# Values and transposed weights of key blocks with one query tile: split float32r products in shared banks

## The chip, the cores and the metric

The kernel runs on one core of a Trainium2 chip, as one program. The metric is the device time of one execution in microseconds. TensorE does the matrix products and the transposes and writes PSUM; ScalarE (ACT in the rows), VectorE (DVE) and GpSimd (POOL) do the rest; SyncE (SP) issues the transfers.

## What is computed

A trunk of two layers on 1024 tokens of width 1024. The first layer mixes tokens by dilated sliding-window attention: 16 heads of 64, and three groups with a window and a dilation each; the groups' outputs are merged by a softmax over their log-sum-exps. The second layer is a state-space layer with its own projections. All inputs and outputs are float32. The part that matters:

```python
DILATED_GROUPS = ((128, 1), (512, 4), (2048, 16))
def dilated_group_attention(q, k, v, rel_bias, window, dilation):
    # query t attends to t - j*dilation, j = 0..window/dilation
    ...
    logits = jnp.einsum('bnqrhe,bnkrhe->bnrhqk', qs, kw) * scale + bias
    logits = jnp.where(valid[None, :, None, None], logits, NEG)
    lse = jax.nn.logsumexp(logits, axis=-1)
    p = jnp.exp(logits - lse[..., None])
    o = jnp.einsum('bnrhqk,bnkrhe->bnqrhe', p.astype(v.dtype), vw)
    ...
def dilated_attention_mixer(h, w_in, w_out, rel_bias):
    ...
    wts = jax.nn.softmax(jnp.stack(lses), axis=0)
    o = jnp.sum(wts[..., None] * jnp.stack(outs).astype(jnp.float32), axis=0)
    ...
    return (o * jax.nn.silu(z)) @ w_out
```

## The kernel before

The program has stages one after the other: norm and values of all groups, written to DRAM (until some 343 us of the profiled span); attention (343 to 1165 us); gate and output projection; the state-space layer; its gate and the last projection.

Attention runs over 8 pairs of heads (`attn_pair`, L665), in each over the three groups, in each over two units of four query tiles of 128 (`attn_unit`, L472). For a group, queries and keys are projected (`proj_half`, L114; the products stand on L110), brought out of PSUM and split. To split (`split`, L79) means: ScalarE writes a tile rounded to float32r (L83), VectorE or GpSimd subtracts it from the source to get the rest (L84). A product of near float32 precision is then made of two or three float32r products of the parts.

`load_v` (L444) brings the values of a pair and group, eight key blocks of 128 tokens with two heads of 64, from DRAM into `vp` (L454; two buffers) and splits them into `vs` (one buffer): rounded part in 64 columns, rest in the next 64, so one product with 128 columns of weights gives both halves, and the two halves of the result are added when it leaves PSUM (L582, L583). In groups 0 and 1 only the blocks listed in `SPLIT_BLOCKS` (L226) are split: six of eight in group 0, four in group 1. These are the blocks that serve two query tiles of a unit.

In a unit, the logits of a query tile are products of the split queries and keys (L495), 256 columns wide, or 128 where a query tile has a single key block. VectorE adds the bias and takes the row maximum (L498), ScalarE takes the exponential (L509). Then `pv_first` (groups 0 and 1) or `pv_last` (group 2) makes the products with the values. `pv_first` goes head by head: blocks of weights are transposed by TensorE into a PSUM bank (`transposed`, L516; pool of two banks, tile `pt`), the bank is split into `ph` (`split_weights`, L524; two buffers), and each key block with two query tiles gets two products of 256 columns, rounded and rest, with `vs` (L572). Key blocks with one query tile in the unit are transposed into a bank of their own (tile `ptp`), copied by ScalarE to the float32 tile `pf` (L568) and multiplied with the raw `vp` as plain float32 products with 64 columns of weights and 128 columns (L572 too, operands `pf,vp`). In a unit and head these are two key blocks (unit 0 of group 0, both units of group 1) or one (unit 1 of group 0). All products of a head and unit accumulate in one bank, in the order of the list `jobs`.

The order on each engine is set at build time: a scheduler takes ready instructions by priority along a simulated time line, and some steps (weight loads and splits, evictions of projections) are put ahead by `AHEAD`. On the chip each engine and the SP queue keep that order and wait by semaphores. Weights of a projection come through `load_w` (L90, load on L95), the bias tile through `load_bias` (L180, L186).

Of the kernel before, what the change touches and what calls it, by code (L numbers as in the profile page):

```python
# [15 lines left out]
F32 = mybir.dt.float32  # L16
F32R = mybir.dt.float32r
# [6 lines left out]
P = 128  # L24
S = 1024
D = 1024
KT = 8
H = 512
# [192 lines left out]
        c.nc.gpsimd.tensor_copy(t[rows, s, :], c.zt[rows].to_broadcast([64, S]))  # L221

SPLIT_BLOCKS = ((0, 1, 2, 4, 5, 6), (0, 2, 4, 6), (0, 1, 2, 3, 4, 5, 6, 7))  # L226


def load_first(c, a, k):
    raw = c.wraw.tile([P, 2, H], F32, tag="wraw", name="wvr")  # L230
    c.nc.sync.dma_start(raw, a["w_v"][0, k // 2])
# [212 lines left out]
def load_v(c, p, g):  # L444


    nc = c.nc
    vp = c.attn.tile([P, KT, P], F32, tag="vp", name="vp", bufs=2)
    o = ORD[g]
    off = c.v_dr.offset + (g * 2 + p // 4) * S * H + p % 4 * P  # L450

    for dst, at, step in (((vp, 0, P),), ((vp[:, 0::2], 0, 1), (vp[:, 1::2], o * P, 1)), ((vp, 0, 1),))[g]:
        src = bass.AP(c.v_dr.tensor, off + at * H, [[o * H, P], [step * H, dst.shape[1]], [1, P]])
        nc.sync.dma_start(dst, src)  # L454
    vs = c.attn.tile([P, KT, 2, P], F32R, tag="vs", name="vs", bufs=1)
    if g == 2:
        split(c, vs[:, :, 0], vs[:, :, 1], vp)
        return vp, vs
    src = vp.rearrange("p b (h d) -> p b h d", h=2)
    nb = len(SPLIT_BLOCKS[g])  # L460
    for n, blocks in enumerate((slice(0, 3), slice(4, 7)) if g == 0 else (slice(0, 8, 2),)):
        dst = vs[:, 3 * n:3 * n + 3] if g == 0 else vs[:, 0:nb]
        split(c, dst[:, :, :, 0:64], dst[:, :, :, 64:128], src[:, blocks])
    return vp, vs


def ms_col(g, n, h, qt):
# [4 lines left out]
def attn_unit(c, g, u, q, k, v, bt, ms, O):  # L472


    nc = c.nc
    qh, ql = q
    kh, kl = k
    vp, vs = v
    lg = c.attn.tile([P, 2, 4, 256], F32, tag="lg", name="lg", bufs=3)
    tiles = []  # L480
    for j in range(4):
        qt = u * 4 + j
        m = (7 - qt, 1 - qt % 2, 0)[g]
        start = (max(m - 1, 0) * P, qt // 2 * 256, qt * P)[g]
        w = 256 if m else 128
        tiles.append(w)
        ps = c.psl.tile([P, 2, 256], F32, tag="psl", name="psl")
        qs = slice(qt * P, qt * P + P)
        ks = slice(start, start + w)
        if g == 2:  # L490
            jobs = [(ps[:, :, 0:w], a, b[:, :, ks]) for a, b in ((qh, kh), (qh, kl), (ql, kh))]
        else:
            jobs = [(ps[:, h, 0:w], (qh, ql)[h], b[:, h, ks]) for h in range(2) for b in (kh, kl)]
        for n, (o, a, b) in enumerate(jobs):
            nc.tensor.matmul(o, a[:, qs], b, start=n == 0, stop=n == len(jobs) - 1, skip_group_check=True)  # L495
        for h in range(2):
            col = ms_col(g, 0, h, qt)
            nc.vector.tensor_tensor_reduce(  # L498
                lg[:, h, j, 0:w], ps[:, h, 0:w], bt[:, h, 256 - w:256], scale=1.0, scalar=-3.0e38,
                op0=ALU.add, op1=ALU.max, accum_out=ms[:, col:col + 1])  # L500
    nm = c.small.tile([P, 2, 4], F32, tag="nm", name="nm")
    at = (4 - 4 * u, 4 * u, 4 * u)[g]
    mx = ms[:, 0:16].rearrange("p (h t) -> p h t", h=2)[:, :, at:at + 4]
    nc.vector.tensor_scalar(nm, mx, -1.0, None, op0=ALU.mult)  # L504
    for h in range(2):
        for j, w in enumerate(tiles):
            col = ms_col(g, 1, h, u * 4 + j)
            b = (3 - j, j ^ 1, j)[g]
            nc.scalar.activation(lg[:, h, j, 0:w], lg[:, h, j, 0:w], AF.Exp, bias=nm[:, h, b:b + 1],  # L509
                                 accum_out=ms[:, col:col + 1])  # L510
    (pv_last if g == 2 else pv_first)(c, g, u, lg, vp, vs, O)
    if u == 1:
        put_ms(c, g, ms)


def transposed(c, lg, blocks, name):  # L516

    pt = c.pst.tile([P, H], F32, tag="pst", name=name)
    for n, (h, j, part) in enumerate(blocks):
        c.nc.tensor.transpose(pt[:, n * P:(n + 1) * P], lg[:, h, j, part * P:part * P + P], c.ident)  # L520
    return pt


def split_weights(c, pt, wd):  # L524
    t = c.attn.tile([P, 2, H], F32R, tag="ph", name="ph", bufs=2)
    hi, lo = t[:, 0], t[:, 1]
    split(c, hi[:, 0:wd], lo[:, 0:wd], pt[:, 0:wd])
    return hi, lo
# [9 lines left out]
    return O[g]  # L538


def pv_first(c, g, u, lg, vp, vs, O):


    nc = c.nc

    if g == 0:
        sp = [(6 - 4 * u - j, j, [(j, 0), (j + 1, 1 if j < 2 or u == 0 else 0)]) for j in range(3)]
        pl = [(7 - 4 * u, 0, [(0, 1)])]
        if u == 0:
            pl.append((3, 3, [(3, 0)]))  # L550
    else:
        sp = [(4 * u + j, j, [(j, 0), (j + 1, 0)]) for j in (0, 2)]
        pl = [(4 * u + 1 + j, j, [(j, 1)]) for j in (0, 2)]
    for h in range(2):
        po = c.pso.tile([P, H], F32, tag="pso", name="pso")
        jobs = []
        for b0 in range(0, len(sp), 2):
            grp = sp[b0:b0 + 2]
            pt = transposed(c, lg, [(h, j, part) for _, _, parts in grp for j, part in parts], "pt")
            hi, lo = split_weights(c, pt, 256 * len(grp))  # L560
            for n, (kb, col, parts) in enumerate(grp):
                s = slice(256 * n, 256 * n + 256)
                for x in (hi, lo):
                    jobs.append((po[:, col * P:col * P + 256], vs[:, SPLIT_BLOCKS[g].index(kb), h], x[:, s]))
        pt = transposed(c, lg, [(h,) + parts[0] for _, _, parts in pl], "ptp")
        wd = P * len(pl)
        pf = c.slot("pf", F32, tag="a")
        nc.scalar.copy(pf[:, 0:wd], pt[:, 0:wd])  # L568
        for n, (kb, col, parts) in enumerate(pl):
            jobs.append((po[0:64, col * P:col * P + P], vp[:, kb, 64 * h:64 * h + 64], pf[:, n * P:(n + 1) * P]))  # L570
        for n, (o, l, r) in enumerate(jobs):
            nc.tensor.matmul(o, l, r, start=n == 0, stop=n == len(jobs) - 1, skip_group_check=True)  # L572
        out = out_tile(c, g, O)

        rows = HEADS[h]
        if g == 0:
            dst = out[rows].rearrange("p (i n) -> p i n", i=8)[:, :, 64 - 64 * u:128 - 64 * u]
            fr = [po[x, ::-1].rearrange("p (n i) -> p i n", i=8) for x in HEADS]
        else:
            dst = out[rows].rearrange("p (b r n) -> p r b n", b=2, r=4)[:, 2 * u:2 * u + 2]  # L580
            fr = [po[x].rearrange("p (r l) -> p r l", r=2)[:, :, ::-1].rearrange("p r (n b) -> p r b n", b=2) for x in HEADS]
        nc.scalar.copy(dst, fr[0])  # L582
        nc.vector.tensor_tensor(dst, dst, fr[1], op=ALU.add)  # L583


def pv_last(c, g, u, lg, vp, vs, O):


    nc = c.nc
# [1040 lines left out]
```

## Time and profile before

| | us |
|---|---|
| median of 3 runs | 1743.67 |
| lowest, highest | 1740.37, 1746.24 |
| profiled execution | 1741.3 |
| its span, first to last instruction | 1739.5 |
| TensorE busy over the span | 1677.0 (96%) |
| VectorE busy | 1038.2 (60%) |
| ScalarE busy | 797.3 (46%) |
| GpSimd busy | 482.1 (28%) |

The mean granted TensorE clock is 0.991 of full speed. Busy time of TensorE is a sum of modelled spans of products that overlap in the pipeline, so the starts of successive products tell more of its pace than their durations. In the rows, PE is TensorE's products and transposes, PEld its weight loads; L572 is line 572 of the kernel; `out<-in,in` are tiles by the program's names, the moving operand ahead of the weights.

### The profile page before, as it was taken

To read this page: it belongs to the slowest core of one execution; us is meant where nothing else is said; L and a number is where in the kernel's file an instruction comes from. 1 tells how busy PE (TensorE), PEld (TensorE's weight loads), DVE (VectorE), ACT (ScalarE), POOL (GpSimd) and SP (SyncE) were. 2 spreads that over 40 slices of the span, in tenths; PEclk is the share of its full clock that TensorE was granted. 3 is DMA by queue.
4 is the path that set the end of the run, shared out by engine and by line. 5 is a ranking of instruction groups with operands and counts; after the bars stand their busy time and mean duration, and the time that the engine had idled before them with its cause. 6 is when DMAs were issued, how large, how long until landed. Compare 5 with 4: busy or idle time off the path is not lost. (4 is left out here: it accounts for less than half of the span.)

```text
span 1739.5 us, 25821 instructions
## 1 busy us (share of the span) xinstructions
PE 1677.0 (96%) x9262; PEld 1414.2 (81%) x9262; DVE 1038.2 (60%) x2558; ACT 797.3 (46%) x1912; POOL 482.1 (28%) x321
## 2 busy tenths in 40 slices
PE   6999999999999999999999999998998999989998
PEld 5889999987878888788888888886886888867886
DVE  7698898634555556455564656467462677764533
ACT  5232222246656656666666756653352232233411
POOL 2000000132242332424253252405120344423121
PEclk9999999999999999999999999998999999999999
DMA  6223455441233223223232332427249866455432
GB/s 233 90 52 100 145 170 152 143 125 53 77 86 88 76 80 100 77 81 95 80 85 92 101 94 63 131 71 200 82 140 243 216 214 221 135 176 175 140 122 85
DMA packets 176900, 212.68 MB, mean 122 GB/s; under 512 B 37361, under 2 KB 133380, under 8 KB 176772
## 3 DMA queue, kind: packets, MB, share of 16 engines
q1 hardware_dynamic: 176772, 211.04, 40.7%
q8 instruction: 73, 1.20, 0.3%
q14 instruction: 55, 0.45, 0.1%
HBM read 154.03 MB, written 56.96 MB: 121 GB/s over the span
## 5 line engine op out<-in xcount | busy, mean ns | idle before, releaser
L110 PE MATMUL psj<-hh,whi 128*128 128x512 f32 x896 | 359.9, 402 | 7.3 <-DVE tz L814 3.8
L110 PE MATMUL psj<-hl,whi 128*128 128x512 f32 x896 | 357.5, 399 | 0.0
L110 PE MATMUL psj<-hh,wlo 128*128 128x512 f32 x896 | 356.3, 398 | 0.2 <-POOL wlo L84 0.2
L84 POOL TENSOR_TENSOR wlo<-wraw,whi 128x1024 fp32r<-128x1024 f32 x48 | 115.3, 2402 | 377.5 <-ACT whi L83 365.3
L110 PEld LDWEIGHTS psj<-hh,whi 128*128 128x128 f32 x896 | 169.4, 189 | 43.6 <-ACT kh L214 5.9
L110 PEld LDWEIGHTS psj<-hh,wlo 128*128 128x128 f32 x896 | 169.3, 189 | 36.4 <-POOL wlo L84 0.6
L110 PEld LDWEIGHTS psj<-hl,whi 128*128 128x128 f32 x896 | 169.6, 189 | 32.5
L509 ACT ACTIVATE lg<-lg,nm 128x128 f32<-128x128 f32 (+1 forms) x384 | 168.0, 440 | 22.9 <-DVE nm L504 22.2
L498 DVE CUSTOM_DVE_ANT_0 lg<-psl,T 128x128 f32<-128x128 f32 (+1 forms) x384 | 117.3, 348 | 91.1 <-PE psl L495 89.2
L83 ACT CAST whi<-wraw 128x1024 fp32r<-128x1024 f32 x80 | 83.8, 1048 | 147.0 <-PE psj L110 105.1
L394 PE MATMUL psq<-whi,v 128*128 128x256 f32 x640 | 118.7, 283 | 0.0
L110 PE MATMUL psj<-h1h,whi 128*128 128x512 f32 (+1 forms) x272 | 107.4, 395 | 11.3 <-DVE z L1415 7.9
L84 DVE TENSOR_TENSOR kl<-psj,kh 64x512 fp32r<-64x512 f32 x96 | 66.0, 687 | 76.0 <-ACT kh L83 75.7
L84 DVE TENSOR_TENSOR ph<-pt,ph 128x512 fp32r<-128x512 f32 (+1 forms) x128 | 78.7, 621 | 52.8 <-ACT ph L83 51.5
L110 PE MATMUL psj<-h1l,whi 128*128 128x512 f32 (+1 forms) x272 | 105.8, 389 | 0.2 <-DVE h1l L84 0.2
L110 PE MATMUL psj<-h1h,wlo 128*128 128x512 f32 (+1 forms) x272 | 105.4, 388 | 0.0
L394 PEld LDWEIGHTS psq<-whi,v 128*128 128x128 f32 x640 | 99.6, 189 | 1.0 <-ACT whi L83 0.6
L394 PE MATMUL psq<-wlo,v 128*128 128x256 f32 x320 | 90.7, 284 | 1.6 <-DVE wlo L84 1.6
L1231 POOL TENSOR_TENSOR Ks<-Ks,O 32x64 f32<-32x64 f32 x8 | 4.6, 572 | 296.8 <-ACT Ks L1229 281.1
L83 ACT CAST whi<-v 128x1024 fp32r<-128x1024 f32 x35 | 36.8, 1052 | 101.5 <-PE psq L394 74.2
L897 POOL TENSOR_TENSOR xr<-xr,y 128x512 f32<-128x512 f32 x30 | 38.1, 1292 | 139.0 <-DVE y L896 100.3
L520 PE MATMUL pt<-identr,lg 128*128 128x128 f32 x448 | 75.3, 278 | 0.2 <-ACT lg L509 0.2
(292 smaller groups left out, 4013.3 us busy)
## 6 DMA issues: line engine op xcount, KB each, us to landing
wraw<-in_w_in_dram SPq DMA_DIRECT2D x56, 512.0 KB
mw<-wt_dr SPq DMA_DIRECT2D x48, 256.0 KB
v<-in_w_v_dram SPq DMA_DIRECT2D x20, 512.0 KB
vp<-v_dr SPq DMA_DIRECT2D x16, 512.0 KB
wraw<-in_ssm_w_in_dram SPq DMA_DIRECT2D x16, 512.0 KB
v_dr<-v SPq DMA_DIRECT2D x30, 256.0 KB
rot_dr<-rt SPq DMA_DIRECT2D x48, 128.0 KB
ca_dr<-ca SPq DMA_DIRECT2D x32, 144.0 KB
```

Of the source, the lines that this page charges most:

```text
L83: nc.scalar.copy(hi, src)
L84: return (engine or nc.vector).tensor_tensor(lo, src, f32(hi), op=ALU.subtract)
L110: nc.tensor.matmul(ps, a[:, s], b[:, k, :], start=first and k == 0 and n == 0, stop=k == KT - 1 and n == 2, skip_group_check=True)
L394: nc.tensor.matmul(o, r[x][:, k, ts], w[y][:, k, :], skip_group_check=True, start=i in (0, 4, 5) and t % 2 == k == n == 0, stop=k == 3 and ...
L498: nc.vector.tensor_tensor_reduce(lg[:, h, j, 0:w], ps[:, h, 0:w], bt[:, h, 256 - w:256], scale=1.0, scalar=-3.0e38, op0=ALU.add, op1=ALU.m ...
L509: nc.scalar.activation(lg[:, h, j, 0:w], lg[:, h, j, 0:w], AF.Exp, bias=nm[:, h, b:b + 1], accum_out=ms[:, col:col + 1])
L520: c.nc.tensor.transpose(pt[:, n * P:(n + 1) * P], lg[:, h, j, part * P:part * P + P], c.ident)
L897: nc.gpsimd.tensor_tensor(x[:, ns], x[:, ns], y, op=ALU.add)
L1231: nc.gpsimd.tensor_tensor(Ks[:, :, 0:16], Ks[:, :, 0:16], self.dd, op=ALU.add)
```

## The change

Every key block of groups 0 and 1 is now split, in one piece of 1024 columns for each part, as in group 2; `SPLIT_BLOCKS` goes. Key blocks with one query tile are multiplied as split products: two float32r products of 128 columns with `vs` take the place of one plain product with `vp`. Their transposed weights go through the same eviction (`split_weights`) as the others: in group 0 they share the second bank with the third block of two tiles (512 columns in unit 0, 384 in unit 1), in group 1 they have the second bank to themselves (256 columns). The tiles `ptp` and `pf` are gone. `ph` gets three buffers in place of two, `vp` one in place of two.

```diff
--- before.py
+++ after.py
@@ -219,11 +219,6 @@
     for s in range(2):
         rows = HEADS[1 - s]
         c.nc.gpsimd.tensor_copy(t[rows, s, :], c.zt[rows].to_broadcast([64, S]))
-
-
-
-
-SPLIT_BLOCKS = ((0, 1, 2, 4, 5, 6), (0, 2, 4, 6), (0, 1, 2, 3, 4, 5, 6, 7))
 
 
 def load_first(c, a, k):
@@ -445,7 +440,7 @@
 
 
     nc = c.nc
-    vp = c.attn.tile([P, KT, P], F32, tag="vp", name="vp", bufs=2)
+    vp = c.attn.tile([P, KT, P], F32, tag="vp", name="vp", bufs=1)
     o = ORD[g]
     off = c.v_dr.offset + (g * 2 + p // 4) * S * H + p % 4 * P
 
@@ -455,13 +450,9 @@
     vs = c.attn.tile([P, KT, 2, P], F32R, tag="vs", name="vs", bufs=1)
     if g == 2:
         split(c, vs[:, :, 0], vs[:, :, 1], vp)
-        return vp, vs
-    src = vp.rearrange("p b (h d) -> p b h d", h=2)
-    nb = len(SPLIT_BLOCKS[g])
-    for n, blocks in enumerate((slice(0, 3), slice(4, 7)) if g == 0 else (slice(0, 8, 2),)):
-        dst = vs[:, 3 * n:3 * n + 3] if g == 0 else vs[:, 0:nb]
-        split(c, dst[:, :, :, 0:64], dst[:, :, :, 64:128], src[:, blocks])
-    return vp, vs
+    else:
+        split(c, vs[:, :, :, 0:64], vs[:, :, :, 64:128], vp.rearrange("p b (h d) -> p b h d", h=2))
+    return vs
 
 
 def ms_col(g, n, h, qt):
@@ -475,7 +466,6 @@
     nc = c.nc
     qh, ql = q
     kh, kl = k
-    vp, vs = v
     lg = c.attn.tile([P, 2, 4, 256], F32, tag="lg", name="lg", bufs=3)
     tiles = []
     for j in range(4):
@@ -508,7 +498,7 @@
             b = (3 - j, j ^ 1, j)[g]
             nc.scalar.activation(lg[:, h, j, 0:w], lg[:, h, j, 0:w], AF.Exp, bias=nm[:, h, b:b + 1],
                                  accum_out=ms[:, col:col + 1])
-    (pv_last if g == 2 else pv_first)(c, g, u, lg, vp, vs, O)
+    (pv_last if g == 2 else pv_first)(c, g, u, lg, v, O)
     if u == 1:
         put_ms(c, g, ms)
 
@@ -522,7 +512,7 @@
 
 
 def split_weights(c, pt, wd):
-    t = c.attn.tile([P, 2, H], F32R, tag="ph", name="ph", bufs=2)
+    t = c.attn.tile([P, 2, H], F32R, tag="ph", name="ph", bufs=3)
     hi, lo = t[:, 0], t[:, 1]
     split(c, hi[:, 0:wd], lo[:, 0:wd], pt[:, 0:wd])
     return hi, lo
@@ -538,36 +528,33 @@
     return O[g]
 
 
-def pv_first(c, g, u, lg, vp, vs, O):
+def pv_first(c, g, u, lg, vs, O):
 
 
     nc = c.nc
 
     if g == 0:
-        sp = [(6 - 4 * u - j, j, [(j, 0), (j + 1, 1 if j < 2 or u == 0 else 0)]) for j in range(3)]
-        pl = [(7 - 4 * u, 0, [(0, 1)])]
+        first = [(6 - 4 * u - j, j, [(j, 0), (j + 1, 1 if j < 2 or u == 0 else 0)]) for j in range(3)]
+        single = [(7 - 4 * u, 0, [(0, 1)])]
         if u == 0:
-            pl.append((3, 3, [(3, 0)]))
+            single.append((3, 3, [(3, 0)]))
+        banks = [first[:2], first[2:] + single]
     else:
-        sp = [(4 * u + j, j, [(j, 0), (j + 1, 0)]) for j in (0, 2)]
-        pl = [(4 * u + 1 + j, j, [(j, 1)]) for j in (0, 2)]
+        banks = [[(4 * u + j, j, [(j, 0), (j + 1, 0)]) for j in (0, 2)],
+                 [(4 * u + 1 + j, j, [(j, 1)]) for j in (0, 2)]]
     for h in range(2):
         po = c.pso.tile([P, H], F32, tag="pso", name="pso")
         jobs = []
-        for b0 in range(0, len(sp), 2):
-            grp = sp[b0:b0 + 2]
-            pt = transposed(c, lg, [(h, j, part) for _, _, parts in grp for j, part in parts], "pt")
-            hi, lo = split_weights(c, pt, 256 * len(grp))
-            for n, (kb, col, parts) in enumerate(grp):
-                s = slice(256 * n, 256 * n + 256)
+        for bank in banks:
+            blocks = [(h, j, part) for _, _, parts in bank for j, part in parts]
+            wd = P * len(blocks)
+            hi, lo = split_weights(c, transposed(c, lg, blocks, "pt"), wd)
+            at = 0
+            for kb, col, parts in bank:
+                n = P * len(parts)
                 for x in (hi, lo):
-                    jobs.append((po[:, col * P:col * P + 256], vs[:, SPLIT_BLOCKS[g].index(kb), h], x[:, s]))
-        pt = transposed(c, lg, [(h,) + parts[0] for _, _, parts in pl], "ptp")
-        wd = P * len(pl)
-        pf = c.slot("pf", F32, tag="a")
-        nc.scalar.copy(pf[:, 0:wd], pt[:, 0:wd])
-        for n, (kb, col, parts) in enumerate(pl):
-            jobs.append((po[0:64, col * P:col * P + P], vp[:, kb, 64 * h:64 * h + 64], pf[:, n * P:(n + 1) * P]))
+                    jobs.append((po[:, col * P:col * P + n], vs[:, kb, h], x[:, at:at + n]))
+                at += n
         for n, (o, l, r) in enumerate(jobs):
             nc.tensor.matmul(o, l, r, start=n == 0, stop=n == len(jobs) - 1, skip_group_check=True)
         out = out_tile(c, g, O)
@@ -583,7 +570,7 @@
         nc.vector.tensor_tensor(dst, dst, fr[1], op=ALU.add)
 
 
-def pv_last(c, g, u, lg, vp, vs, O):
+def pv_last(c, g, u, lg, vs, O):
 
 
     nc = c.nc
```

## Rows read from the trace of the kernel before

**Rows 1.** Windows: stretch, its length; busy us (count) by engine; clock; DMA share, GB/s.

```profile
343.00:1165.00 822.00, 812.35 (x4416) 675.84 (x4415) 432.73 (x1308) 508.67 (x1410) 293.32 (x163) 1.00 0.31 88
```

**Rows 2.** Waits of TensorE in 343:1165: who waits <- for whom, total us, times, longest.

```profile
PE pso L572 <- ACT ph L83: 4.2, 3, 1.9
```

**Rows 3.** Lines by shape, 343:1165: group, xcount | busy us, mean ns | idle before it.

```profile
L572 PEld LDWEIGHTS pso<-ph,vs 128*128 128x128 f32 x320 | 49.9, 191 | 9.4 <-ACT ph L83 4.8
...
L572 PEld LDWEIGHTS pso<-pf,vp 128*64 128x64 f32 x224 | 22.7, 136 | 12.3 <-issue 4.1 <-ACT kh L83 1.1 <-ACT pf L568 0.7
```

**Rows 4.** TensorE's timeline at 599 and 619 us: start, us, operation, xcount of merged records.

```profile
599.39 0.39 PE L110 MATMUL psj<-hl,whi 128*128 128x512 f32 x1
599.62 0.40 PE L110 MATMUL psj<-hh,wlo 128*128 128x512 f32 x1
599.95 0.65 PE L572 MATMUL pso<-pf,vp 128*64 128x128 f32 x4
600.53 0.44 PE L520 MATMUL pt<-identr,lg 128*128 128x128 f32 x2
...
619.62 0.43 PE L572 MATMUL pso<-pf,vp 128*64 128x128 f32 x2
619.98 0.44 PE L520 MATMUL pt<-identr,lg 128*128 128x128 f32 x2
```

**Rows 5.** TensorE's timeline at 623 us, logits of a tile with one key block.

```profile
623.42 0.22 PE L495 MATMUL psl<-kh,qh 128*128 128x128 f32 x1
623.48 0.28 PE L495 MATMUL psl<-kl,qh 128*128 128x128 f32 x1
623.59 0.28 PE L495 MATMUL psl<-kh,ql 128*128 128x128 f32 x1
623.70 0.27 PE L495 MATMUL psl<-kl,ql 128*128 128x128 f32 x1
623.81 0.45 PE L110 MATMUL psj<-hh,whi 128*128 128x512 f32 x1
```

**Rows 6.** Lines by shape, 343:1165: evictions of transposed weights, splits of values.

```profile
L84 DVE TENSOR_TENSOR ph<-pt,ph 128x512 fp32r<-128x512 f32 x95 | 65.2, 688 | 50.8 <-ACT ph L83 49.8
...
L83 ACT CAST ph<-pt 128x512 fp32r<-128x512 f32 x95 | 55.3, 585 | 13.4 <-PE pt L520 12.0
...
L568 ACT COPY pf<-ptp 128x256 f32<-128x256 f32 x48 | 17.9, 373 | 6.3 <-PE ptp L520 6.0
...
L84 DVE TENSOR_TENSOR ph<-pt,ph 128x256 fp32r<-128x256 f32 x32 | 13.5, 421 | 1.8 <-ACT ph L83 1.4
L83 ACT CAST ph<-pt 128x256 fp32r<-128x256 f32 x32 | 11.9, 372 | 0.2
L84 DVE TENSOR_TENSOR vs<-vp,vs 128x1024 fp32r<-128x1024 f32 x8 | 11.3, 1409 | 2.3 <-ACT vs L83 2.2
...
L83 ACT CAST vs<-vp 128x1024 fp32r<-128x1024 f32 x8 | 8.4, 1044 | 1.8 <-PE pso L572 1.8
...
L84 DVE TENSOR_TENSOR vs<-vp,vs 128x512 fp32r<-128x512 f32 x8 | 6.1, 765 | 24.0 <-ACT vs L83 24.0
L83 ACT CAST vs<-vp 128x512 fp32r<-128x512 f32 x8 | 4.9, 617 | 2.9 <-PE pso L572 2.9
```

**Rows 7.** Timeline, first pair, from group 0's last products to group 1's first.

```profile
423.01 0.28 PE L572 MATMUL pso<-ph,vs 128*128 128x256 f32 x1
...
423.98 0.69 DVE L84 TENSOR_TENSOR vs<-vp,vs 128x512 fp32r<-128x512 f32 x1 [2.51 <-ACT vs L83]
...
425.82 0.43 PE L572 MATMUL pso<-pf,vp 128*64 128x128 f32 x2
...
431.77 0.28 PE L572 MATMUL pso<-ph,vs 128*128 128x256 f32 x1
```

**Rows 8.** Timeline: SP's loads of values, and the next split of group 0.

```profile
459.23 2.04 SPq L454 DMA_DIRECT2D vp<-v_dr  x3
...
477.55 1.02 DVE L84 TENSOR_TENSOR vs<-vp,vs 128x384 fp32r<-128x384 f32 x2
```

## The prediction

> **What bounds the kernel now.** Only the attention stretch, 343 to 1165 us of the span, runs the code that is changed, so I read that stretch first, in the view that sums each engine over a window. TensorE is busy for 812 of its 822 us at the full granted clock, ScalarE for 509, VectorE for 433, GpSimd for 293 [rows 1]. The reader is to see one engine without room and three with a third or more to spare. A busy TensorE may be waiting between pipelined products, so next comes the list of its waits in that stretch: the longest is 4.2 us, on the ScalarE half of a split of transposed weights [rows 2]. All its idle time there is 10 us [rows 1]. So what counts is how long TensorE takes to issue its stream, and the starts of successive products are the measure, not their durations, which overlap.
>
> **The plain products that go.** For each of 8 pairs the two first groups have, per head and unit, one run of plain float32 products with 64 columns of weights. By the loops that is 6 runs of two products and 2 runs of one in a pair, 48 and 16 in the kernel, 112 products. The trace shows each product as two records, 224 of them [rows 3]. The neighbouring 512-column products start 0.23 us apart; from the last of them to the run of two there are 0.33 us, and from the run's start to the next instruction 0.58 us [rows 4]. So a run of two takes 0.33 - 0.23 + 0.58 = 0.68 us of TensorE. A run of one takes 0.36 us from its start [rows 4], and with the same 0.10 us ahead of it 0.46 us. Sum: 48 x 0.68 + 16 x 0.46 = 40.0 us.
>
> **The split products that come.** Each plain product becomes two float32r products of 128 columns, with all 128 columns of weights: four in a run where there were two, two where there was one, 224 in all. The same shape exists in the logits of the tiles with a single key block: four in a row start 0.06, 0.11 and 0.11 us apart, and the next instruction follows after another 0.11 us [rows 5]. The first one is short because its weights had come in behind a longer product; the others wait for theirs. A run of four takes 0.39 us, one of two 0.17 us: 48 x 0.39 + 16 x 0.17 = 21.4 us. If each paid 0.11 us it would be 24.6 us, if each were hidden behind longer products 0.06 x 224 = 13.4 us. I take 21.4, since the new runs follow 256-column products as those in the rows follow theirs. **TensorE gains 40.0 - 21.4 = 18.6 us**, with bounds of 15.4 and 26.6.
>
> The number of transposes stays at 560: blocks only move from a bank of their own into a shared one. That saves one bank in three in the first group, and the pool has two; it may relieve some of the waits, and I count nothing for it.
>
> **ScalarE and VectorE.** Per pair and head, the first unit of group 0 trades two ScalarE evictions of 256 columns (0.37 us each) for one wider part (0.59 in place of 0.37 us), so it saves 0.16 us; the second unit trades much the same; in group 1 a cast replaces the copy at the same price [rows 6]. ScalarE therefore stays where it was. VectorE gets work that did not exist: in group 1 a 256-column subtraction of 0.42 us for each of 32 heads and units; in group 0 subtractions that are wider by 256 columns (0.69 against 0.42) 16 times, and by 128, about half of that, 16 times. That is 13.4 + 4.3 + 2.1, about 20 us [rows 6]. The values are split in one piece of 1024 columns, also in group 1 (1.04 for 0.62 us on ScalarE, 1.41 for 0.77 on VectorE) [rows 6], which adds 8 x 0.64, some 5 us, to VectorE, and little in group 0, where two pieces become one. VectorE goes from 433 to about 460 of 822 us. As it is never what TensorE waits for by name [rows 2], I cost this at nothing. What hides it is TensorE's projection products of the next groups; uncovered, the 0.42 us at each of 64 units and heads would be 27 us.
>
> **The split values, one buffer.** They are written once TensorE has read the last of the group before. In the first pair the last split product of group 0 starts at 423.0, the last plain one at 425.8, as the plain one reads the raw values, not the split ones. After the change it reads the split values too, and the next split may begin only then, 2.8 us later. It is also longer by 0.43 + 0.64 us [rows 6], together 3.9 us. The subtraction ended at 424.7 and the next reader started at 431.8 [rows 7], 7.1 us later. In the eight pairs this slack is 3.1 to 7.1 us, and in six of them the release moves by about 0.5 us, not by 2.8. So it fits, and I cost it at nothing. Queued behind the split are, on ScalarE and VectorE, the exponentials and row maxima of the next unit.
>
> **The raw values, one buffer in place of two.** The load of a group now waits until the group before it has been split. Now three loads go out together at 459.2, two of them for group 1 of the next pair; after the change those two wait for the split of group 0, which ends at 478.6 [rows 8]. Group 1 needs them only after all of group 0's products, nearly 50 us later, so the landing is hidden. The queue is SP's, and weight and bias loads stand behind a load that waits. If the queue keeps its order, up to 478.6 - 459.2 = 19 us of a held queue would come in each pair; a weight load that far behind would stop TensorE for some of it. An order planned with the new wait puts the load later, so I take nothing. The third buffer for split weights only removes waits. Memory stays equal: one 4 KB buffer goes, one comes.
>
> **Sum.** The profiled execution's span is 1739.5 us and its own time 1741.3; 1741.3 - 18.6 = 1722.7 us. The median of the runs is 1743.67, 2.4 us more; on it the same sum gives 1725.1 us. I take **1725 us**.
>
> **A rule on weight loads.** The busy time of weight loads in the stretch is 676 of 822 us [rows 1], and the change puts 224 loads of 191 ns in place of 224 of 136 ns [rows 3], 12.3 us more. The Trainium skill, Perfetto Trace Analysis, section Identifying the Most-Contended Engine, judges TensorE's headroom by the busy share of weight loads and not by that of products. By that measure the change would be a loss. The first of the rivals below is this one, as a mechanism.
>
> **Rivals.**
> Weight side: if loads of weights set TensorE's pace everywhere, those 12.3 us come on top: 1756 us. Against it: loads of 0.19 us lie under products 0.23 us apart [rows 3, 4]; only in runs of 128 columns do they set the pace, and that is in the sum.
>
> Switching stays: at the column rate of the neighbours (0.23 us for 512) four passes of 128 columns take 0.23 us, two products 0.47, so 0.21 of the 0.68 us are entry and exit. If that belongs to the transposes that follow and not to the plain products, 64 x 0.21 = 13.4 us stay, the gain is 5.2 us and the time 1738.5. The four passes of a true float32 product are stated by the Trainium skill, FP8 and Floating Point Precision, section TensorE Precision Notes; the trace has two records, whose time goes beyond four passes. Against the rival: plain products add 0.10 us on entry already, before any transpose [rows 4].
>
> Handover of the split values, **the one that ends slower**: eight times, between groups 0 and 1, readers start 3.9 us later, 31 us in all, and 1743.7 - 18.6 + 31 = 1756 us. It decides once the delay exceeds the 3.1 to 7.1 us of slack, which happens if the new order puts the readers right behind the split as the old plan had it and VectorE's queue is full. Half exposed, 15.6 us, it gives 1741, no difference.
>
> More than the sum: products hidden at 0.06 us (26.6 us) and the 4.2 us of waits on the weights' split gone: some 31 us, 1713.
>
> **Chances.** Forecast, 1720 to 1730: 0.55. More than the sum, 1711 to 1720: 0.14. Switching stays, about 1738.5, on the edge of 0.3%: 0.06, half to each side. Handover or held queue half exposed, 1733 to 1748: 0.18, of which 0.05 on the fast side of 0.3%. Handover fully exposed: 0.05. Weight side: 0.02. About 0.3%, 5.2 us, is what a measurement of this kernel can tell from no change. Faster by over 0.3% (under 1738.4): 0.55 + 0.14 + 0.03 + 0.05 = 0.77. Within: 0.13 + 0.03 = 0.16. Slower: 0.05 + 0.02 = 0.07. The range goes from 1713, the far end of the gain, to 1741, the handover half exposed; some 0.15 lies above it and little below.
>
> **What would show it.** TensorE's records fall by 224 of the plain kind and rise by 224 of 128 columns; runs of the latter take 0.39 us or less and the stretch of attention shrinks by 15 to 27 us with TensorE still at 98% or more of it. The stages before and after keep their lengths to within 2 us. Wrong would be: new waits of TensorE on the split values or on VectorE's half of the split weights, a held SP queue with TensorE waiting for a weight split, or an attention stretch of about the old length with fewer busy microseconds in it.

## The result and the profile after

The changed kernel takes 1725.7 us (median of 4 runs, 1722.9 to 1727.7) against 1743.2 us before; the ratio is 0.9898, with a 95% interval of 0.9876 to 0.9921. The forecast was 1725. The sum holds nearly to the microsecond, but the profile shows that it is made of other parts than those I had added up, and most of what follows is about that.

Engines over the span, from the page of the kernel after:

```profile
span 1721.1 us, 25792 instructions
...
PE 1655.9 (96%) x9262; PEld 1415.1 (82%) x9262; DVE 1064.8 (62%) x2582; ACT 799.9 (46%) x1872; POOL 483.5 (28%) x321
```

VectorE has 26.6 us more in the whole span, ScalarE 2.6 us more, in line with the steps that cost them. The stretch of attention in the view by windows, which answers to [rows 1], is cut 18 us earlier here; the last product with values starts at 1156.2 us, 14.7 us earlier than before (1170.9):

```profile
343.00:1147.00 804.00, 792.30 (x4406) 676.93 (x4406) 452.22 (x1329) 509.17 (x1367) 294.38 (x163) 1.00 0.32 90
```

The waits of TensorE there (total us, times, longest), which answer to [rows 2]:

```profile
PE psj L110 <- ACT kh L214: 8.5, 4, 2.6
PE pso L559 <- ACT ph L83: 1.5, 1, 1.5
PE pso L559 <- DVE ph L84: 1.3, 3, 0.6
PE psj L110 <- POOL wlo L84: 0.3, 1, 0.3
```

and two more rows of the same list in the kernel before:

```profile
PE psj L110 <- ACT kh L214: 3.5, 6, 1.4
PE ptp L520 <- DVE ph L84: 0.5, 2, 0.3
```

The reader is to see that the waits on split weights have become shorter, from 4.2 us on ScalarE's half and 0.5 on VectorE's to 1.5 and 1.3, and that another one has grown: projection products wait for ScalarE's copy of the projected keys (L214), which cost 3.5 us in the kernel before and now costs 8.5.

Lines by shape in the same stretch, the counterparts of [rows 6] and of the plain products in [rows 3]:

```profile
L559 PE MATMUL pso<-ph,vs 128*128 128x128 f32 x224 | 35.5, 257 | 0.0
...
L84 DVE TENSOR_TENSOR vs<-vp,vs 128x1024 fp32r<-128x1024 f32 x24 | 29.4, 1224 | 6.5 <-ACT vs L83 5.8
...
L83 ACT CAST vs<-vp 128x1024 fp32r<-128x1024 f32 x24 | 25.2, 1050 | 4.3 <-DMA vp<-v_dr 4.0
...
L84 DVE TENSOR_TENSOR ph<-pt,ph 128x256 fp32r<-128x256 f32 x32 | 13.5, 422 | 5.4 <-ACT ph L83 4.8
...
L84 DVE TENSOR_TENSOR ph<-pt,ph 128x384 fp32r<-128x384 f32 x16 | 8.9, 555 | 0.1
```

One run of group 1 in TensorE's timeline, three products of 256 columns and four of 128, merged into one line that bears the shape of its first, and the transposes behind it; this answers to [rows 4, 5]:

```profile
438.68 0.91 PE L559 MATMUL pso<-ph,vs 128*128 128x256 f32 x7
439.43 0.84 PE L510 MATMUL pt<-identr,lg 128*128 128x128 f32 x6
```

From start to start that is 0.75 us. Three products of 256 columns take 3 x 0.118 us, so the four new ones take 0.40 us, where the sum had 0.39. The transposes follow without a further delay. Of the 48 runs of four, 23 stand whole like this one; in the other 25 the planned order puts other records between the products. All 224 together take 21.0 us from start to start.

The handover in the first pair, which answers to [rows 7], and SP's loads of values, which answer to [rows 8]:

```profile
419.59 0.45 PE L559 MATMUL pso<-ph,vs 128*128 128x256 f32 x3
...
423.47 1.22 DVE L84 TENSOR_TENSOR vs<-vp,vs 128x1024 fp32r<-128x1024 f32 x1
...
428.65 0.28 PE L559 MATMUL pso<-ph,vs 128*128 128x256 f32 x1
```

```profile
459.62 0.39 SPq L449 DMA_DIRECT2D vp<-v_dr  x1
...
481.32 1.24 SPq L449 DMA_DIRECT2D vp<-v_dr  x2
```

The subtraction ends at 424.7 and the next reader starts at 428.7, 4.0 us later. The two loads for group 1 have moved from 460 to 481 us, behind the split of group 0, and need to be there only some 40 us later.

**Issue time and holes.** To find where the time went I take TensorE's stream from the first product of the logits to the last product with values, and compare the distance between the starts of two successive records with the median distance for the same kinds of record (the one before, this one, the one after), taken over all kernels of this study. What lies over the median by more than 60 ns is called a hole here, the rest issue time. Holes include short delays that the list of waits doesn't name, and the wider spacing where the granted clock falls (1.2 us before, 1.4 after). A kind is the tile that is written and the shape, with the transposes into `pt` and `ptp` counted as one; with the operands told apart as well, the kernel before has 788.3 us of issue time and 13.4 of holes, so the division between the two is good to some 2 us. As some projection products of the next stage are placed inside or behind this stretch, the issue time is brought to the same number of them, 2304, at 0.2335 us each.

| kernel | median us | stretch | issue time | holes |
|---|---|---|---|---|
| before | 1743.2 | 797.5 | 786.6 | 15.0 |
| after | 1725.7 | 783.3 | 766.4 | 16.9 |

The change took 20.2 us of issue time and added 1.9 us of holes. The kernel before has 18 projection products behind the stretch that the kernel after has inside it, 4.2 us. So the stretch is shorter by 20.2 - 1.9 - 4.2 = 14.1 us, by the two lengths 14.2.

The 18 products had covered part of a chain that follows. From the last product with values to the first product of the output projection there are 26.3 us before and 26.7 after: the outputs of the last pair are weighted, merged and split there, and TensorE waits. The waits from 1160 us on, before:

```profile
PE pso L868 <- ACT gh L83: 3.8, 1, 3.8
PE psj L110 <- DVE tz L814: 3.4, 1, 3.4
```

and after, from 1147 us on:

```profile
PE psj L110 <- DVE tz L801: 7.7, 1, 7.7
PE pso L855 <- ACT gh L83: 3.0, 1, 3.0
```

So moving them early gave nothing back. The spans differ by 18.4 us. Besides the 14.2, attention starts 0.5 us earlier, and from the last product with values to TensorE's last record it is 560.1 us before and 556.4 after. Most of these 3.7 us, 3.2, lie in the first 20 us of the output projection, where a wait is 0.8 us shorter and the clock differs. Windows of the chain and of the 45 us behind it, in the kernel before and in the kernel after:

```profile
1171.00:1205.00 34.00, 30.58 (x126) 24.36 (x125) 26.79 (x46) 19.44 (x43) 12.19 (x6) 0.95 0.80 219
1205.00:1250.00 45.00, 41.24 (x171) 32.86 (x170) 20.24 (x64) 10.92 (x28) 16.18 (x7) 0.92 0.29 94
```

```profile
1156.00:1190.00 34.00, 26.35 (x107) 21.08 (x106) 27.69 (x46) 19.62 (x45) 10.86 (x6) 0.90 0.80 219
1190.00:1235.00 45.00, 42.04 (x185) 33.67 (x184) 22.49 (x74) 12.26 (x30) 16.49 (x8) 1.00 0.29 94
```

In the 45 us the granted clock is 0.92 before and 1.00 after: 7 us were at the lower of the two levels, 1.2 GHz, which costs up to half of them. In the chain ahead it is the other way round, 0.95 before and 0.90 after, and there TensorE waits for a part of the time. So the clock fell in both kernels, and in the kernel after at a cheaper place. This is a matter of one profiled execution; with the medians, 17.5 us, it can't be told apart.

### The profile page after: what moved, and what is told of

It reads as the page before. It is cut to its first block, busy times and chain, and to the rows that moved or that the text cites. A ratio compares the mean times of both kernels' runs of the same rounds, so it can differ in the third digit from the quotient of the medians.

```text
span 1721.1 us, 25792 instructions
## 1 busy us (share of the span) xinstructions
PE 1655.9 (96%) x9262; PEld 1415.1 (82%) x9262; DVE 1064.8 (62%) x2582; ACT 799.9 (46%) x1872; POOL 483.5 (28%) x321
## 5 line engine op out<-in xcount | busy, mean ns | idle before, releaser
L84 DVE TENSOR_TENSOR ph<-pt,ph 128x512 fp32r<-128x512 f32 (+2 forms) x160 | 97.2, 621 | 37.4 <-ACT ph L83 35.3
L570 DVE TENSOR_TENSOR O<-O,pso 64x512 f32<-64x512 f32 x64 | 44.2, 691 | 103.3 <-ACT O L569 102.6
L83 ACT CAST ph<-pt 128x512 fp32r<-128x512 f32 (+2 forms) x160 | 81.6, 533 | 35.9 <-PE pt L510 34.7
L510 PE MATMUL pt<-identr,lg 128*128 128x128 f32 x560 | 93.5, 275 | 0.0
L559 PE MATMUL pso<-ph,vs 128*128 128x256 f32 (+1 forms) x544 | 89.9, 275 | 2.8 <-ACT ph L83 1.5
L559 PEld LDWEIGHTS pso<-ph,vs 128*128 128x128 f32 x544 | 81.6, 189 | 13.1 <-ACT ph L83 2.6
```

Source lines behind the costliest of these rows:

```text
L83: nc.scalar.copy(hi, src)
L84: return (engine or nc.vector).tensor_tensor(lo, src, f32(hi), op=ALU.subtract)
```

## The experiments

All are compared with the kernel before, run beside them; its median in those sessions was 1740.9 to 1744.0 us. The table has what the traces gave; the sections below say what each tells apart. The planner gives each of these kernels an order of its own, but for the one with the old buffers, which keeps the order of the kernel after on TensorE, ScalarE, VectorE and GpSimd. So an edit is tested together with the order that it brings.

| kernel | median us | ratio to before, 95% | issue time | holes |
|---|---|---|---|---|
| rounded part only | 1702.3 | 0.9762 (0.9737 to 0.9786) | 754.4 | 6.5 |
| plain twice, on before | 1766.9 | 1.0137 (1.0108 to 1.0166) | 811.2 | 19.0 |
| group 1 only | 1744.4 | 1.0007 (0.9993 to 1.0022) | 776.2 | 29.6 |
| group 0 only | 1742.3 | 0.9998 (0.9985 to 1.0012) | 776.8 | 22.3 |
| before, reordered | 1750.0 | 1.0049 (1.0033 to 1.0065) | 786.9 | 21.2 |
| after, reordered | 1724.7 | 0.9893 (0.9868 to 0.9919) | 766.2 | 17.6 |
| after, old buffers | 1725.4 | 0.9894 (0.9856 to 0.9932) | 766.3 | 19.8 |
| after, longer split | 1722.1 | 0.9878 (0.9851 to 0.9905) | 767.0 | 15.8 |
| after, copy on VectorE | 1710.3 | 0.9817 (0.9795 to 0.984) | 765.9 | 2.5 |
| after, own bank | 1751.0 | 1.0045 (1.0027 to 1.0063) | 765.9 | 47.4 |
| before, copy on VectorE | 1724.8 | 0.99 (0.9878 to 0.9922) | 786.2 | 2.6 |
| own bank, copy on VectorE | 1730.4 | 0.9928 (0.9911 to 0.9946) | 765.5 | 23.7 |

Whatever the order and the holes, the seven kernels that make all products of the change have 765.5 to 767.0 us of issue time, and the three with the products of before have 786.2 to 786.9.

### What a product costs

```diff
--- after
-                for x in (hi, lo):
+                for x in (hi, lo)[:len(parts)]:
```

> The changed kernel without the products of the rest of the weights for key blocks with one query tile: 112 of the 224 new products are left out (the contribution of that rest is missing from the output); everything else, the evictions too, stays. Theory (TensorE's issue is the bound, a new product costs what the trace of the changed kernel shows, 21.0 us for 224, 94 ns each): 10.5 us less than the changed kernel's 1725.7, about 1715 us. Rival, weight loads set the pace: 112 loads of 189 ns, 21 us less, about 1705. Rival, TensorE's stream is not what sets the time (the evictions or the splits do): no difference, 1726.

It took 1702.3 us, 23.4 less than the changed kernel, close to what weight loads as the pace would give and not to my theory. The decomposition says otherwise: issue time fell by 12.0 us, 0.107 us for each of the 112 products left out, and holes fell by 10.4 us, from 16.9 to 6.5. The theory of issue had 10.5 for the first part and nothing for the second, and weight loads as the pace would have been 21 us of issue time. Read by its total alone, this run would have confirmed the wrong rival.

```diff
--- before
-            jobs.append((po[0:64, col * P:col * P + P], vp[:, kb, 64 * h:64 * h + 64], pf[:, n * P:(n + 1) * P]))
+            for _ in range(2):
+                jobs.append((po[0:64, col * P:col * P + P], vp[:, kb, 64 * h:64 * h + 64], pf[:, n * P:(n + 1) * P]))
```

> The kernel before with every plain product issued twice in a row (what key blocks with one query tile contribute is counted twice in the output). Theory (a run has a price for entering and leaving, and a record inside it costs 0.13 us): 224 records more inside the runs, 29 us more than before, about 1772 us. Rival, each plain product costs the same wherever it stands (40 us for 112): 40 us more, about 1783. Rival, products are hidden behind other engines: 1743.

It took 1766.9 us, 25 us more than before in that session, 24.6 us of it issue time: 0.22 us for each plain product that is added inside a run. A run of two thus costs two of these, 0.44 us, and 0.24 us on top, for entering and leaving; the rival with one price for every product (40 us) falls. The theory's 29 us were too many as well: a record inside a run costs 0.11 us in the trace, not 0.13. The Trainium skill, FP8 and Floating Point Precision, section TensorE Precision Notes, has a true float32 product make four passes; at the neighbours' 0.23 us for 512 columns that makes an estimate of 0.23 us, which the 0.22 bears out for a product inside a run.

### One group alone

The two kernels give the code of the change to one group and leave the other group's and the buffers as before.

```diff
--- before
-SPLIT_BLOCKS = ((0, 1, 2, 4, 5, 6), (0, 2, 4, 6), (0, 1, 2, 3, 4, 5, 6, 7))
+SPLIT_BLOCKS = ((0, 1, 2, 4, 5, 6), (0, 1, 2, 3, 4, 5, 6, 7), (0, 1, 2, 3, 4, 5, 6, 7))
...
+        if g == 1:
+            banks = [sp, pl]
+            for bank in banks:
...
-        for b0 in range(0, len(sp), 2):
+        else:
+            for b0 in range(0, len(sp), 2):
...
```

> Only group 1 is changed (values split in one piece, split products for key blocks with one query tile, in a bank of their own as in the change); group 0 and the buffers stay as before. Theory: 32 runs of two plain products go, 32 x (0.68 - 0.38) = 9.6 us, about 1734 us. Rival, the gain comes from the shared banks and the third bank saved in group 0: 1743 here. Rival, the longer split of the values between groups 0 and 1 shows without the new buffers: over 1740.

> Only group 0 is changed (values split in one piece, split products, shared banks); group 1 and the buffers stay as before. Theory: 16 runs of two and 16 of one go, 16 x (0.68 - 0.38) + 16 x (0.46 - 0.17) = 9.4 us, about 1734 us. Rival, the shared banks bring more, as ScalarE has fewer evictions ahead of what TensorE waits for at the start of a pair: 1726 to 1730, nearly the whole gain.

Neither is faster: 1744.4 and 1742.3 us, ratios of 1.0007 and 0.9998. Both theories fell. For group 1 alone the times of the two rivals came out (1743, over 1740), but not their reasons: the kernel with group 0 alone has the shared banks and gains nothing either, so its own rival (1726 to 1730) falls with them, and no row of the waits names the split of the values. Issue time, on the other hand, fell by 10.4 and by 9.8 us, where the theory had 9.6 and 9.4, and the two together make the 20.2 of the whole change. Holes ate the gains, all of the one and most of the other: 29.6 and 22.3 us, against 15.0 before. The waits of TensorE in the kernel with group 1 alone (343 to 1140 us):

```profile
PE psj L110 <- ACT kh L214: 8.5, 11, 1.4
PE pso L588 <- ACT ph L83: 7.1, 6, 1.6
PE pso L614 <- ACT ph L83: 2.8, 5, 0.6
```

They name ScalarE, as before and after do. So the question was no longer why the change gains, but what makes the holes, since they decide whether a gain of issue time arrives.

### Order, buffers, handover

```diff
--- before
-AHEAD = 600
+AHEAD = 300
```

> The kernel before with the lead of urgent steps (AHEAD) at 300 in place of 600: the same instructions, planned in another order on TensorE, VectorE and ScalarE. Theory (time is TensorE's issue time plus holes where it waits for ScalarE or VectorE, and the holes belong to the order, not to the change): issue time of the attention stretch as before, 786 us to within 3, and holes that differ from before's 15 us by several us either way, the time by as much: 1735 to 1756. Rival (holes belong to the tiles and waits, whatever the order): holes within 3 us of before's, time 1743 to within 4.

1750.0 us: the same work in another order, slower by 0.5%, issue time 786.9 us as before, 6.2 us more in holes. Order alone moves the kernel's time by about as much as one of the halves saves in issue time.

```diff
--- after
-AHEAD = 600
+AHEAD = 150
```

> The changed kernel with the lead of urgent steps (AHEAD) at 150 in place of 600: the same instructions in another order. Theory (holes belong to the order): issue time of the attention stretch as in the changed kernel, 766 us to within 3, holes between 6 and 28 us, where the changed kernel has 17: 1715 to 1737. Rival (the changed tiles and buffers keep the holes at 17 us): 1726 to within 4.

1724.7 us, issue time 766.2, holes 17.6. That lies in the range of both the theory and the rival and does not tell them apart.

```diff
--- after
-    vp = c.attn.tile([P, KT, P], F32, tag="vp", name="vp", bufs=1)
+    vp = c.attn.tile([P, KT, P], F32, tag="vp", name="vp", bufs=2)
...
-    t = c.attn.tile([P, 2, H], F32R, tag="ph", name="ph", bufs=3)
+    t = c.attn.tile([P, 2, H], F32R, tag="ph", name="ph", bufs=2)
```

> The changed kernel with the buffers of before: two for the raw values, two for the split transposed weights. TensorE, VectorE and ScalarE keep the very order of the changed kernel, only the SP queue differs. Theory (buffers are no part of it): 1726 us to within 3. Rival (the third buffer of split weights is what kept the holes at 17 us where the kernels with one changed group, with two buffers, have 22 and 28): 5 to 11 us more, 1731 to 1737.

1725.4 us: the buffers of the change are no part of its effect. That speaks against the third buffer of split weights as what the one-group kernels lacked; these two were not run with it. With the order of the compute engines unchanged, this is also the cleanest repetition of the change itself: 0.9894.

```diff
--- after, in load_v behind the split
+    hi, lo, src = ((vs[:, :, 0], vs[:, :, 1], vp) if g == 2 else
+                   (vs[:, :, :, 0:64], vs[:, :, :, 64:128], vp.rearrange("p b (h d) -> p b h d", h=2)))
+    nc.vector.tensor_tensor(lo, src, f32(hi), op=ALU.subtract)
```

> The changed kernel with the subtraction that splits the values done twice, 24 more of 1.22 us on VectorE, 29 us in all, each in the handover from one group to the next. Theory (the handover and VectorE's added work lie beside TensorE's stream): issue time 766 us, the time moves by holes of another order alone, 1718 to 1735. Rival (the handover is on the path): up to 24 x 1.2 = 29 us more, 1745 to 1755.

1722.1 us, no slower. The second subtraction is there, 24 of 1.25 us (30.0 us of VectorE), and TensorE's list of waits names no split of values. In an order that is planned for it, the handover lies beside the stream.

### What makes the holes

One of the longest holes after, in TensorE's timeline:

```profile
593.61 0.39 PE L110 MATMUL psj<-hh,wlo 128*128 128x512 f32 x1
596.56 0.50 PE L110 MATMUL psj<-hh,whi 128*128 128x512 f32 x1 [2.57 <-ACT kh L214]
```

and what ScalarE does meanwhile (the last of seven exponentials in a row, which begin at 591.86):

```profile
594.72 0.49 ACT L499 ACTIVATE lg<-lg,nm 128x256 f32<-128x256 f32 x1
...
595.33 0.58 ACT L569 COPY O<-pso 64x512 f32<-64x512 f32 x1
595.93 0.58 ACT L214 CAST kh<-psj 64x512 fp32r<-64x512 f32 x1
```

The next projection needs the PSUM bank that the copy of the keys frees; the copy stands in ScalarE's order behind seven exponentials and an eviction. There are 64 such copies of 0.58 us. To take them out of that line:

```diff
--- after
-            c.nc.scalar.copy(dh[HEADS[1 - s]], sv[HEADS[s]])
+            c.nc.vector.tensor_copy(dh[HEADS[1 - s]], sv[HEADS[s]])
```

> The changed kernel with the second copy of the projected keys (L214, 64 copies of 0.58 us) on VectorE in place of ScalarE. Theory (the holes come from ScalarE, where this copy waits in line behind exponentials; TensorE names it for 8.5 us): issue time 766 us, holes down from 17 to 8 to 12 us, about 1718 us. Rival (VectorE, with 37 us more, becomes what TensorE waits for): holes of 17 us or more with VectorE as the releaser, 1726 or more.

1710.3 us: holes fall from 16.9 to 2.5 us, further than the 8 to 12 expected, and issue time stays at 765.9. VectorE is busy for 511 us of the 807 from 343 on:

```profile
343.00:1150.00 807.00, 797.75 (x4453) 683.44 (x4452) 510.83 (x1418) 480.74 (x1321) 294.66 (x164) 1.00 0.32 93
```

and up to 1140 us TensorE does not wait for it by name; the whole list of its waits there is

```profile
PE pt L510 <- ACT lg L499: 0.7, 1, 0.7
PE pso L559 <- ACT ph L83: 0.5, 1, 0.5
```

This version keeps the whole computation and beats both kernels, by 1.8% the one before. The same edit, on the kernel before:

> The kernel before with the second copy of the projected keys (L214) on VectorE in place of ScalarE. Theory (issue time belongs to the work, holes to ScalarE's line): issue time 786 us as before, holes down from 15 to 2 to 8 us, time 1728 to 1738; against the changed kernel with the same edit (1710.3) that leaves 18 to 25 us, TensorE's issue time of the change almost alone. Rival (the edit helps the changed kernel alone): no change, 1742.

1724.8 us, issue time 786.2, holes 2.6. These two are as the theory had them; the time is 3 us under its range. The copy alone on the old products is worth what the whole change is worth. Between the two kernels with the copy on VectorE the holes are equal, so their difference in the stretch is the issue time of the change without disturbance: 20.3 us. In the medians 14.5 us arrive, where 18 to 25 were expected: 4.2 us lie in the 18 moved products again, as the chain behind the last pair takes 27.5 and 27.7 us, and the clock takes some more. In the profiled executions the stages behind the stretch are 7.1 us longer in the changed kernel, with a granted clock of 0.86 over the chain and 0.93 over the 50 us behind it, against 0.95 and 1.00; the mean clock of its four runs is 0.987 to 0.991, against 0.992 to 0.995. How much of the medians that is was not separated.

### The shared bank

```diff
--- after
-        banks = [first[:2], first[2:] + single]
+        banks = [first[:2], first[2:], single]
```

> The changed kernel without the shared bank in group 0: blocks with one query tile have a bank of their own again, so three evictions per head there in place of two, on ScalarE and on VectorE. Theory (sharing saves evictions beside TensorE's stream): issue time 766 us, the time moves by holes of another order, 1718 to 1737. Rival (sharing the bank is what carries the gain, by one wait less per head on a pool of two banks): holes up by 10 us or more, over 1736.

1751.0 us, slower than the kernel before. The issue time is that of the change, 765.9 us; the holes are 47.4. So without the shared bank, in the order planned for it, the whole gain and 9 us more are lost, and my theory that sharing only saves evictions beside the stream fell. What TensorE waits for (343 to 1150 us):

```profile
PE psj L110 <- ACT kh L214: 13.6, 7, 2.0
PE pso L559 <- DVE vs L84: 6.3, 5, 1.3
PE psj L110 <- DVE ql L201: 4.3, 6, 0.7
PE pso L559 <- ACT ph L83: 2.0, 1, 2.0
```

The second row is the handover of the split values, the rival that was to end slower: in this order it does reach TensorE.

All waits of TensorE that the profile names in this kernel's stretch come to 29 us, not 47. Another 8.6 us of the holes are products issued at the lower clock: in six places, 20 us in all, the granted clock falls to 1.2 GHz, each time right behind a wait of 2.0 us. In one of them (the mean clock from 700 to 710 us is 0.83) 512-column products start 0.42 us apart in place of 0.23:

```profile
700.56 0.50 PE L110 MATMUL psj<-hh,whi 128*128 128x512 f32 x1 [2.04 <-ACT kh L214]
...
702.19 0.63 PE L110 MATMUL psj<-hh,wlo 128*128 128x512 f32 x1
702.61 0.63 PE L110 MATMUL psj<-hh,whi 128*128 128x512 f32 x1
```

The kernels before and after have one such place each in the stretch, and none with the copy of the keys on VectorE. So a wait can cost more than its own length.

With both edits, own banks and the copy of the keys on VectorE:

> The changed kernel with a bank of their own for blocks with one query tile in group 0 and the second copy of the projected keys on VectorE. Theory (the 47 us of holes of the kernel with own banks come from ScalarE's line, not from the pool of two banks): holes 3 to 15 us, 1711 to 1725. Rival (three banks per head on a pool of two make TensorE wait whatever ScalarE does): holes stay over 30 us, 1737 or more.

1730.4 us, holes 23.7. Both expectations missed: with the copy moved half of the 47 us go, and the other half stays, with VectorE and ScalarE named for it (343 to 1150 us):

```profile
PE psj L110 <- DVE ql L201: 8.1, 5, 1.7
PE pso L559 <- ACT kh L83: 4.8, 4, 1.2
```

With own banks there are 32 more evictions of split weights on each of the two engines, and TensorE's order is another one; which of the two makes the remaining 21 us over the shared bank (2.5) was not separated. A third bank per head on the pool of two is not enough by itself: the kernel before has it too in group 0, there with a copy on ScalarE alone, and with the copy of the keys on VectorE it leaves 2.6 us.

## Why the prediction came out right

**The main step held.** Plain products were to cost 40.0 us and their successors 21.4, a gain of 18.6. Issue time fell by 20.2, and by 20.3 between the two kernels that have the copy on VectorE. A run of four new products that stands whole takes 0.40 us where 0.39 was read off the logits' rows, and all 224 take 21.0 us. Why the first takes 0.06 us and the others 0.11 was argued from the loads and not tested. The 0.24 us of entering and leaving a run of two that the doubled plain products leave over are gone: transposes follow the new runs without them. So the rival "switching stays" falls. The gain is 1.6 us over the sum, which is within what the choice of kinds moves it by.

**The weight side** was not the pace. Issue time fell by 0.107 us for each product left out, and not by the 0.19 us of its load. I had worked out 12.3 us more of loads and set them beside a busy time. The busy time over the span barely moved, from 1414.2 to 1415.1 us, as loads of 0.19 us stand 0.11 us apart in the new runs and the profile's busy time counts an overlap once. (That holds for the products too; it is no sum of their spans.) The durations of all loads in the trace add up to 1695.4 us before and 1707.1 after, 11.7 more and close to my 12.3; the issue time fell by 20.2 all the same. The Trainium skill, Perfetto Trace Analysis, section Identifying the Most-Contended Engine, judges how near TensorE is to its limit by that sum as a share of the time. The share rises from 97 to 99% of the span here; it does not price the change.

**ScalarE and VectorE** came out as costed: ScalarE +2.6, VectorE +26.6 us over the span, and of the longer subtractions and the handover TensorE's list shows 1.3 us on VectorE's half of the split weights, where 0.5 stood before. That is small, but it is one of the signs that I had named for being wrong. Doubling the split of the values by 30 us cost nothing. The single buffer of raw values cost nothing, nor did the queue stop.

**Holes came out alike, and the sum had no reason for it.** The sum carried the old waits over unchanged, and they came out 15.0 and 16.9 us. That they did is luck. The runs show that it was a matter of the order: the same products leave 16 to 47 us of holes, or 2.5, with the order, the banks and the place of a copy. The two halves of the change lose their gain to holes, 14.6 us more than before against 10.4 and 7.3 against 9.8, and the change with own banks loses more than it gains. A range of 28 us around the forecast took in the right case, but its upper end was worked out from the handover alone. Another order of the old products (1750.0 us) and the change with own banks (1751.0) ended slower mostly by other waits than those of the rivals I named, so 0.07 for a slower kernel looks too low.

**Two readings of the waits were loose.** The 4.2 us were the total of three waits, the longest of them 1.9. And VectorE was named in the list of before, with 0.5 us on the split weights, where I wrote that it never was. The 4.2 us enter the rival "more than the sum" alone, where the total is the right figure; the second reading stood behind counting VectorE's work as nothing.

**The shared bank** was counted at nothing. That is the step that the runs contradict most: in the two kernels without it holes are 30.5 and 21.2 us more than in their counterparts with it, and the time is 1751.0 and 1730.4 us against 1725.7 and 1710.3. How much of that is the order was not separated.

**Where the gain ends.** I expected the stretch to shrink by 15 to 27 us and the stages behind it to keep their length to within 2 us. Both were missed. The stretch shrank by 14.2, since 18 projection products moved into it, where they no longer covered the chain behind the last pair; the stages behind came out 3.7 us shorter in the profiled execution, mostly by the clock of the output projection. In this pair of executions the two nearly cancel, and the 1.6 us of more gain go against the 1.9 of more holes. So that the total fits to the microsecond is luck; that the gain is some 20 us of issue time is not.

## What to carry to other kernels

On an engine that is busy all the time, the spacing of starts in rows of the same shape, with what it costs to enter and leave a run, forecast the change in issue time to within a tenth (18.6 for 20.2 us). It doesn't forecast the holes, and where a planner sets the order, these move by as much as the change is worth; so split a measured difference into issue time and holes before crediting a cause, and look first for a short eviction that frees a bank behind a row of long operations. Test a change in the form without its helper steps as well: here the gain of the products did not arrive in the kernel without the shared bank, nor with one group alone.

## What was not expected of the hardware

A plain float32 product of 128 columns takes 0.22 us inside a run, yet a run of two costs 0.68 us between float32r products and transposes, as entering and leaving it take about 0.24 us together. Transposes next to float32r products show no such price (0.11 us from the last new product to the first transpose). And the place where the granted clock falls is not the same: behind waits of 3.4 and 3.8 us the kernel before had 0.95 over the chain and 0.92 over the 45 us of products that follow, while the kernel after, with waits of 7.7 and 3.0 us, had 0.90 and 1.00. What decides it was not tested.
